# Sums and low parts of the feed-forward layers moved from GpSimd to VectorE in a two-layer decoder step

## The chip, the cores and the metric

The kernel runs on one core of a Trainium2 chip. The metric is the device time of one execution in microseconds; the time before is the median of three runs. A core has a matrix engine (TensorE, PE in the profile), three engines for elementwise work (VectorE = DVE, ScalarE = ACT, GpSimd = POOL), and queues that issue transfers (SyncE = SP, and here GpSimd too). Each engine works through its own instructions strictly in the order in which they stand; between engines they wait for each other by semaphores. SBUF is the working memory that all of them read; TensorE writes its results to PSUM, which VectorE and ScalarE read.

## The reference

One inference step of a two-layer decoder: 1024 new prompt tokens and 8 tokens of running sequences, model width 1024. Layer 0 has an mLSTM mixer, layer 1 latent attention with a paged cache, and after each mixer comes a dense SwiGLU feed-forward network (width 2816), where the change lies:

```python
def swiglu(x, w_gate_up, w_down):
    g, u = jnp.split(x @ w_gate_up, 2, axis=-1)
    return (jax.nn.silu(g) * u) @ w_down
...
hp = hp + swiglu(rmsnorm(hp, norm_ffn[layer]), ffn_w_gate_up[layer], ffn_w_down[layer])
```

Everything is float32.

## The kernel before

**Precision.** TensorE multiplies in a rounded format (fp32r). Each operand is therefore split in two: a high part, rounded by ScalarE (L117, the helper `split`), and a low part, source minus high part, which an elementwise engine makes at L118. A product is three matmuls: high by high (L134), high by low of the activations (L135), low of the weights by high (L136). `split` takes the engine of the low part as an argument; VectorE is the default.

**Seven products in place of eight.** The tokens are in four column groups: i = 0 and i = 1, of two halves each, 256 wide for i = 0 and 260 for i = 1 (`PW`). Both the gate/up product and the down product are made in 2x2 blocks with seven block products, of sums and differences of the blocks (`PRODUCTS`, in the order 0, 4, 3, 1, 2, 5, 6). So sums of weights and of activations have to be made, and split, ahead of the products:

- `operands` (L987 and following, per row block f of 128 rows, 22 of them): loads two weight tiles `wr` (L994, by SP), makes sums `S` on GpSimd (L1007, L1008, L1012, L1015), and splits seven weight operands.
- `gate_up`: for each f, seven products times two token groups, results in PSUM tiles `sc`; VectorE and ScalarE combine them into `u` (L1047 to L1061). The last product of an f completes `u[:, 1]` at L1061.
- `spread`: for a pair of row blocks (f0, f0+1), combinations of the four blocks of `u` in place, t1 (L1069), t2 (L1071), t3 (L1073) and t4 (L1075), and the splits into seven operands `b` for each token group. The table `SPREAD` says at which step of the down loop each is made: those of the next pair begin some 12 steps before the pair changes and end 4 steps after it.
- `down_raw`: loads a tile `dr` of down weights (L1087, by SP) and makes four sums `dS` of 128x128 (L1090 to L1093); `down_put` splits them and the raw block into `dA`, `dB`, `dC`, `dD`. Once for each of 4 blocks of output columns per pair and 10 pairs a layer: 40 down blocks a layer.
- `down`: for each down block 14 steps (seven products, two token groups), results in PSUM tiles `mm` and `ss`, combined into `wl` (i = 0) or `st` (i = 1) at L1129 to L1140, and at the end two transfers from GpSimd's queue that add the result to the residual in memory (`x_d`, L1141).
- the last two row blocks take another way (`last`), by plain products; four of their low parts are on GpSimd too.

**Order.** `down` is a generator: `gate_up` advances it by one step after every second k, so that the matmuls of gate/up for row block f stand between those of the down blocks of an earlier pair. A scheduler at compile time then sets the order of each engine's queue from the order of the code, the dependencies and its own estimates of durations; it moves instructions of all engines by some places. In the code before, `spread` has the low parts of operands 3 and 5 and the combination t2 on VectorE, and those of 0, 1, 2, 4, 6 and t1, t3, t4 on GpSimd; `down_raw` has all four sums on GpSimd.

Of the kernel before, what the change touches and what calls it, by code (L numbers as in the profile page):

```python
# [91 lines left out]
class Kern:  # L92
# [438 lines left out]
    def gates(self, p1, pg, gi, lf, bcol):  # L531
# [14 lines left out]
        b = self.t(pg, [8, S], "gb")  # L546
        G = self.t(pg, [8, S], "gG")
        wi = self.t(pg, [8, S], "gw")
# [7 lines left out]
        for c in range(NCK):  # L556
            s = slice(c * L, (c + 1) * L)
            V.tensor_tensor_scan(G[:, s], a[:, s], a[:, s], -BIG, op0=ALU.max, op1=ALU.max)
        ck = lambda x: x.rearrange("h (c l) -> h c l", l=L)
# [4 lines left out]
        V.tensor_copy(bL, last(b))  # L564
        V.tensor_tensor(aL, last(G), bL, op=ALU.add)
        V.memset(mm[:, 0:1], 0.0)
        V.tensor_tensor_scan(mm[:, 1:], bL, aL, 0.0, op0=ALU.add, op1=ALU.max)
        mp = mm[:, 0:NCK].unsqueeze(2).to_broadcast([8, NCK, L])
        V.tensor_tensor(ck(G), ck(G), mp, op=ALU.max)
        V.tensor_tensor(b, b, G, op=ALU.add)  # L570
        nc.scalar.activation(em, b, AF.Exp, scale=-1.0)
        V.tensor_tensor(ck(wi), mp, ck(G), op=ALU.subtract)
        nc.scalar.activation(wi, wi, AF.Exp)
# [488 lines left out]


    def spread(self, f0, n, i):
        V, G = self.nc.vector, self.nc.gpsimd
        a = self.u[f0, i]
        b = self.u.get((f0 + 1, i))
        if n == "t1":
            G.tensor_tensor(a[:, 0], a[:, 1], a[:, 0], op=ALU.subtract)  # L1069
        elif n == "t2":  # L1070
            V.tensor_tensor(a[:, 0], b[:, 1], a[:, 0], op=ALU.subtract)  # L1071
        elif n == "t3":
            G.tensor_tensor(a[:, 1], b[:, 1], a[:, 1], op=ALU.subtract)  # L1073
        elif n == "t4":
            G.tensor_tensor(b[:, 0], b[:, 0], a[:, 0], op=ALU.subtract)  # L1075
        else:
            x = a[:, n // 2] if n < 4 and n != 3 else a[:, 0] if n == 3 else b[:, n // 6]
            w = self.t(self.fp, [P, 2, PW[i]], f"b{n}{i}", F32R)
            self.split(w[:, 0], w[:, 1], x, lo_eng=V if n in (3, 5) else G)
            self.B[n, i] = w  # L1080


    def down_raw(self, wd, f0, dp):
        nc = self.nc
        G = nc.gpsimd.tensor_tensor
        raw = self.t(self.fp, [P, 2, 2 * P], "dr")
        nc.sync.dma_start(raw, self.wsrc(wd, f0 * P, 2, dp * 2 * P, 2 * P))  # L1087
        a11, a21, a12, a22 = (raw[:, k, r * P:r * P + P] for k in range(2) for r in range(2))
        S = self.t(self.fp, [P, 4, P], "dS")
        G(S[:, 1], a21, a22, op=ALU.add)  # L1090
        G(S[:, 0], S[:, 1], a11, op=ALU.subtract)
        G(S[:, 2], a11, a21, op=ALU.subtract)
        G(S[:, 3], a12, S[:, 0], op=ALU.subtract)  # L1093
        return {"A": raw[:, :, 0:P], "B": S[:, 0:2], "C": S[:, 2:4], "D": raw[:, 1:2, P:]}
# [59 lines left out]
    def ffn(self, layer):  # L1154
        wg, wd = self.ffn_w_gate_up[layer], self.ffn_w_down[layer]
        self.fp = self.pool("ffn")
        self.B = {}
        for _, x, i in SPREAD:
            if i == 0:
                self.spread(0, x, i)  # L1160
        self.gate_up(wg, 2, (0, 1))
        self.gate_up(wg, 0, (1,))
        self.gate_up(wg, 1, (1,))
        for _, x, i in SPREAD:
            if i == 1:
                self.spread(0, x, i)
        g = self.down(wd)
        next(g)
        self.gate_up(wg, 3, (0, 1), g, 1, 2)
        for f in range(4, NF - 1):  # L1170
            self.gate_up(wg, f, (0, 1), g)
        fs = range(NF - 2, NF)
        self.act = {}

        def last(pool, tag, i):
            for f in fs:
                if f not in self.act:
                    self.act[f] = [self.t(pool, [P, T], tag(f - NF + 2, x), F32R) for x in range(2)]
                o = lambda x: x[:, 512 * i:512 * i + 2 * PW[i]].rearrange("p (c t) -> p c t", c=2)
                self.split(o(self.act[f][0]), o(self.act[f][1]), self.u[f, i], lo_eng=(self.nc.gpsimd, self.nc.vector)[f % 2])  # L1180

        if layer:
            for i in range(2):
                self.gate_up(wg, NF - 1, (i,), g)
                last(self.fz, lambda j, x: f"f{2 * j + x}l", i)
            self.fc.release()
        else:
            self.gate_up(wg, NF - 1, (0, 1), g)
            self.fc.release()
            self.lt = self.pool("lt", side="right")  # L1190
            for i in range(2):
                last(self.lt, lambda j, x: f"l{j}{x}", i)
        for _ in g:
            pass
        return wd, fs
# [822 lines left out]
```

## Time and profile before

| | before |
|---|---|
| time, median of 3 runs | 2898.82 us (2897.31 to 2899.64) |
| profiled execution: time | 2918.12 us |
| profiled execution: span | 2916.0 us |
| mean granted TensorE clock | 0.946 |
| HBM read, written | 255.17 MB, 134.16 MB |

The page gives for each engine its busy time, its share of the span and its number of instructions; other views give the same for a stretch of time (windows), the waits of an engine by what ended them, and the instructions in order of time (timeline: start in us from the span's start, duration in us, engine, source line, operation, tile written <- tiles read, shape, and in brackets the idle time before it with what ended it). A granted clock of 1.00 is full speed. The two feed-forward networks lie at about 540 to 1290 us and 2095 to 2860 us of the span. Names of tiles lose their numbers in the profile.

### The profile page before, as it was taken

The numbers are of one execution on the slowest core, as the hardware profiler recorded it, in microseconds if no ns is written. First come the engines' busy times: TensorE is split into PE (matmuls) and PEld (weight loads), VectorE is DVE, ScalarE is ACT, GpSimd is POOL, SyncE is SP. The second block draws the span as 40 slices with busy tenths as digits, with TensorE's granted clock in tenths as the row PEclk, the third lists the DMA queues.
The fourth block names the chain that finished last, engine by engine and source line by source line (L and its number), as shares of the span: only waits on it lengthen the run. The fifth ranks groups of instructions, "written<-read, shape, count | busy, mean of one in ns | idle before, by whom it ended". The sixth has DMA issues, their size and how long they took to land.

```text
span 2916.0 us, 55167 instructions
## 1 busy us (share of the span) xinstructions
PE 2605.7 (89%) x21199; PEld 2438.1 (84%) x21199; DVE 1891.6 (65%) x3825; ACT 1357.2 (47%) x3403; POOL 1246.2 (43%) x1422
## 2 busy tenths in 40 slices
PE   8999989889889999989888888889979999989987
PEld 8998968889888989988875666677979888989986
DVE  4436678757666666666557777675766676666666
ACT  4213344455545555553354455454445545545543
POOL 1001012356655555542344454433156555555553
PEclk9999989999999999999899999999999999999998
DMA  5134455245555555573666765656316555555555
GB/s 175 44 72 106 120 146 150 80 99 106 113 107 106 106 103 106 114 176 109 215 227 223 262 239 195 204 178 196 120 54 121 102 102 106 112 108 108 113 127 139
DMA packets 346508, 392.91 MB, mean 135 GB/s; under 512 B 23833, under 2 KB 275102, under 8 KB 337926
## 3 DMA queue, kind: packets, MB, share of 16 engines
q0 software_dynamic: 63872, 191.79, 28.5%
q1 hardware_dynamic: 257974, 181.25, 20.9%
q10 hardware_dynamic: 24400, 16.36, 2.1%
q8 instruction: 166, 2.72, 0.4%
q14 instruction: 96, 0.79, 0.1%
HBM read 255.17 MB, written 134.16 MB: 134 GB/s over the span
## 4 chain that ended last, share of the span: by engine, by line
PE 53%; DVE 16%; DMA 10%; POOL 8%; issue 7%; ACT 5%; SPq 0%; another core or an unknown queue 0%; ACTq 0%; POOLq 0%; DVEq 0%
PE sc L134 9%; PE sc L136 9%; PE sc L135 9%; PE mm L134 4%; PE mm L136 4%; PE mm L135 4%; DMA wr<-in_ffn_w_gate_up_dram 3%; POOL b L118 2%; DVE tt L1796 2%; PE ss L1828 2%; DMA Gb<-G_d 2%; PE ss L134 1%; PE ss L135 1%; PE ss L136 1%; DVE b L118 1%
## 5 line engine op out<-in xcount | busy, mean ns | idle before, releaser
L117 ACT ACTIVATE wh<-wr 128x512 fp32r<-128x512 f32 (+3 forms) x176 | 139.0, 790 | 225.9 <-PE mm L135 129.4
L1141 POOL DMA_DIRECT2D x_d<-wl x80 | 96.1, 1202 | 324.0 <-DVE wl L1140 285.4
L118 POOL TENSOR_TENSOR b<-u,b 128x256 fp32r<-128x256 f32 (+1 forms) x200 | 176.5, 918 | 28.8 <-ACT b L117 28.8
L117 ACT ACTIVATE b<-u 128x256 fp32r<-128x256 f32 (+1 forms) x280 | 110.0, 413 | 119.2 <-POOL u L1073 40.1
L1796 DVE STREAM_TRANSPOSE tt<-nat 128x1024 f32<-128x1024 f32 x128 | 154.0, 1223 | 10.0 <-PE ss L1803 6.6
L118 DVE TENSOR_TENSOR wh<-S,wh 128x512 fp32r<-128x512 f32 x121 | 100.9, 834 | 66.1 <-ACT wh L117 65.6
L118 DVE TENSOR_TENSOR b<-u,b 128x256 fp32r<-128x256 f32 (+1 forms) x80 | 115.2, 1454 | 22.7 <-ACT b L117 22.7
L118 DVE TENSOR_TENSOR wl<-wr,wh 128x1024 fp32r<-128x1024 f32 (+2 forms) x83 | 99.2, 1197 | 41.5 <-ACT wh L117 27.3
L1007 POOL TENSOR_TENSOR S<-wr 128x512 f32<-128x512 f32 x45 | 63.7, 1415 | 128.1 <-DMA wr<-in_ffn_w_gate_up_dram 113.1
L1141 POOL DMA_DIRECT2D x_d<-st x80 | 109.4, 1368 | 4.8 <-issue 2.3
L134 PE MATMUL mm<-zh,wh 128*128 128x344 f32 x320 | 104.6, 327 | 5.7 <-DVE ot L462 5.7
L118 DVE TENSOR_TENSOR wh<-wr,wh 128x512 fp32r<-128x512 f32 x91 | 90.5, 996 | 29.4 <-ACT wh L117 28.8
L1803 PE MATMUL ss<-tt,qbd 128*32 128x128 f32 x2560 | 93.5, 281 | 15.9 <-DVE tt L1796 10.5
L135 PE MATMUL mm<-zl,wh 128*128 128x344 f32 x320 | 103.8, 325 | 0.0
L136 PE MATMUL mm<-zh,wl 128*128 128x344 f32 x320 | 103.7, 324 | 0.0
L118 DVE TENSOR_TENSOR dB<-dS,dB 128x256 fp32r<-128x256 f32 x80 | 58.8, 735 | 68.0 <-ACT dB L117 68.0
L1012 POOL TENSOR_TENSOR S<-S,wr 128x512 f32<-128x512 f32 x45 | 63.8, 1417 | 86.8 <-DVE wh L118 66.0
L1803 PEld LDWEIGHTS ss<-tt,qbd 128*32 128x32 f32 x2560 | 72.2, 112 | 32.6 <-DVE tt L1796 18.9
L850 POOL TENSOR_TENSOR ss<-ss,sq 128x512 f32<-128x512 f32 (+2 forms) x36 | 49.4, 1374 | 112.1 <-ACT sq L849 112.0
L117 ACT ACTIVATE wh<-S 128x512 fp32r<-128x512 f32 x121 | 76.2, 630 | 43.0 <-PE sc L136 24.4
L135 PE MATMUL mm<-b,dB 128*128 128x256 f32 (+1 forms) x160 | 48.9, 305 | 46.8 <-DVE b L118 46.8
L130 POOL TENSOR_TENSOR wl<-spl,wh 128x512 fp32r<-128x512 f32 x43 | 54.8, 1285 | 76.7 <-ACT spl L129 72.1
(1028 smaller groups left out, 11543.4 us busy)
## 6 DMA issues: line engine op xcount, KB each, us to landing
wr<-in_ffn_w_gate_up_dram SPq DMA_DIRECT2D x98, 512.0 KB
x_d<-st POOLq DMA_DIRECT2D x80, 520.0 KB
x_d<-wl POOLq DMA_DIRECT2D x80, 512.0 KB
dr<-in_ffn_w_down_dram SPq DMA_DIRECT2D x80, 256.0 KB
wr<-in_mlstm_w_in_dram SPq DMA_DIRECT2D x24, 512.0 KB
wr<-in_mlstm_w_out_dram SPq DMA_DIRECT2D x16, 512.0 KB
wr<-in_mla_w_o_dram SPq DMA_DIRECT2D x15, 512.0 KB
q<-qn_d SPq DMA_DIRECT2D x28, 256.0 KB
```

The costliest lines, as they stand in the source:

```text
L117: ins = nc.scalar.activation(hi, src, AF.Copy)
L118: self.low = e.tensor_tensor(lo, src, hi.bitcast(F32), op=ALU.subtract)
L130: nc.gpsimd.tensor_tensor(lo, x, hi.bitcast(F32), op=ALU.subtract)
L134: mm(ps, wh, xh, start=start, stop=False, **kw)
L135: mm(ps, wh, xl, start=False, stop=False, **kw)
L136: self.last = mm(ps, wl, xh, start=False, stop=stop, **kw)
L1007: G(s, a21, a22, op=ALU.add)
L1012: G(s, s, a11, op=ALU.subtract)
L1141: nc.gpsimd.dma_start(self.x_d[:, 2 * dp:2 * dp + 2, 512 * i:512 * i + 2 * PW[i]], st[i], accum_op=ALU.add)
L1796: V.transpose(out=tt, in_=src.rearrange("p s (c i) -> p c s i", i=32))
L1803: nc.tensor.matmul(psS[32 * j:32 * j + 32, u * P:u * P + P], self.qbd[:, b, cb], tt[:, c, 4 * j:4 * j + 4].rearrange("p s k -> p (s k)"), ...
L1828: nc.tensor.matmul(psV[32 * j:32 * j + 32], pz[:, j, i], keys[i // 4][:, j * 4 + i % 4], start=i == 0, stop=i == 7)
```

## The change

Three places. In `spread`, both names V and G now mean VectorE, and the split's low part is always there: per pair and token group t1, t3, t4 and the low parts of operands 0, 1, 2, 4 and 6. In `down_raw` the four sums are made by VectorE. In `ffn` (function `last`) two low parts per layer and token group, of which one was on GpSimd, are both on VectorE. GpSimd keeps the sums `S` of the gate/up weights and its transfers, and what it does outside these layers. The numbers computed are the same.

```diff
     def spread(self, f0, n, i):
-        V, G = self.nc.vector, self.nc.gpsimd
+        V = G = self.nc.vector
...
             w = self.t(self.fp, [P, 2, PW[i]], f"b{n}{i}", F32R)
-            self.split(w[:, 0], w[:, 1], x, lo_eng=V if n in (3, 5) else G)
+            self.split(w[:, 0], w[:, 1], x, lo_eng=V)
             self.B[n, i] = w
...
     def down_raw(self, wd, f0, dp):
         nc = self.nc
-        G = nc.gpsimd.tensor_tensor
+        G = nc.vector.tensor_tensor
...
-                self.split(o(self.act[f][0]), o(self.act[f][1]), self.u[f, i], lo_eng=(self.nc.gpsimd, self.nc.vector)[f % 2])
+                self.split(o(self.act[f][0]), o(self.act[f][1]), self.u[f, i], lo_eng=self.nc.vector)
```

In all 644 instructions go from GpSimd's queue to VectorE's: 200 low parts of `b`, 120 combinations, 320 sums of `dS` and four low parts of the last row blocks. The order of the engines around them changes with it. Two places are shown, both at the pair change near 1076 us of the profiled execution in layer 0 (u_11339 and u_11375 are the newer row block of the new pair, for the two token groups).

GpSimd's queue before, from the last combination of the pair to the last weight sums of the row block (b are low parts, dS_11786 the sums of the next down block):

```order
L1075 TENSOR_TENSOR u_11375<-u_11375,u_10975 128x260
L1090 TENSOR_TENSOR dS_11786<-dr_11784 128x128
L1092 TENSOR_TENSOR dS_11786<-dr_11784 128x128
L1091 TENSOR_TENSOR dS_11786<-dS_11786,dr_11784 128x128
L118 TENSOR_TENSOR b_11791<-u_10975,b_11791 128x260
L1093 TENSOR_TENSOR dS_11786<-dr_11784,dS_11786 128x128
L118 TENSOR_TENSOR b_11824<-u_11339,b_11824 128x256
L118 TENSOR_TENSOR b_11853<-u_11375,b_11853 128x260
L1012 TENSOR_TENSOR S_11720<-S_11720,wr_11716 128x512
L1015 TENSOR_TENSOR S_11720<-wr_11716,S_11720 128x512
```

GpSimd's queue now, for the same row block and the end of it:

```order
L1007 TENSOR_TENSOR S_11720<-wr_11718 128x512
L1008 TENSOR_TENSOR S_11721<-wr_11716,wr_11718 128x512
L1012 TENSOR_TENSOR S_11720<-S_11720,wr_11716 128x512
L1141 DMA x_d_91<-wl_6158 128x2x512
L1141 DMA x_d_91<-st_11542 128x2x520
L1015 TENSOR_TENSOR S_11720<-wr_11716,S_11720 128x512
L1141 DMA x_d_91<-wl_6157 128x2x512
```

The sums of weights now follow each other with only transfers between them, and L1015, which stood right behind L1012, stands behind two transfers.

VectorE's queue before, from the split of wh_11868 (weight of gate/up product 1) to that of wh_11872 (weight of product 3, made from L1012's sum):

```order
L118 TENSOR_TENSOR wh_11868<-S_11720,wh_11868 128x512
L118 TENSOR_TENSOR dC_11758<-dS_11551,dC_11758 128x256
L118 TENSOR_TENSOR b_11761<-u_10975,b_11761 128x260
L1131 TENSOR_TENSOR wl_6157<-wl_6157,ss_11776 128x256
L118 TENSOR_TENSOR b_11837<-u_11375,b_11837 128x260
L1049 TENSOR_TENSOR u_11765<-u_11765,sc_11813 128x256
L1131 TENSOR_TENSOR st_11777<-st_11777,ss_11779 128x260
L118 TENSOR_TENSOR dA_11884<-dr_11784,dA_11884 128x256
L118 TENSOR_TENSOR wh_11872<-S_11720,wh_11872 128x512
```

VectorE's queue now, the last part of the same stretch:

```order
L1092 TENSOR_TENSOR dS_11786<-dr_11784 128x128
L1091 TENSOR_TENSOR dS_11786<-dS_11786,dr_11784 128x128
L118 TENSOR_TENSOR b_11804<-u_11339,b_11804 128x256
L1093 TENSOR_TENSOR dS_11786<-dr_11784,dS_11786 128x128
L1131 TENSOR_TENSOR wl_6157<-wl_6157,ss_11776 128x256
L118 TENSOR_TENSOR b_11824<-u_11339,b_11824 128x256
L1131 TENSOR_TENSOR st_11777<-st_11777,ss_11779 128x260
L118 TENSOR_TENSOR b_11837<-u_11375,b_11837 128x260
L1049 TENSOR_TENSOR u_11765<-u_11765,sc_11813 128x256
L118 TENSOR_TENSOR b_11853<-u_11375,b_11853 128x260
L1049 TENSOR_TENSOR u_11807<-u_11807,sc_11842 128x260
L118 TENSOR_TENSOR wh_11872<-S_11720,wh_11872 128x512
```

From wh_11868 to wh_11872 there were seven instructions between the two; now there are 24. TensorE's order differs here by a few rows only: behind the first two matmuls with the high part of wh_11872 it now has six of the down product and one of the other token group before the first with the low part. SP's order is the same up to the last block of the program.

## The prediction

> **What bounds the kernel now.** I read the page first: busy time, share of the span and count by engine.
>
> ```profile
> PE 2605.7 (89%) x21199; PEld 2438.1 (84%) x21199; DVE 1891.6 (65%) x3825; ACT 1357.2 (47%) x3403; POOL 1246.2 (43%) x1422
> ```
>
> TensorE bounds it: VectorE and GpSimd are busy at 65% and 43%, so their sums matter only where TensorE stands still. The stretches of down blocks, by engine, come next (window and its length, TensorE, weight load, VectorE, ScalarE, GpSimd, granted clock), then TensorE's longest waits in the second of them (total, times, longest).
>
> ```profile
> 700.00:1280.00 580.00, 531.33 (x4243) 524.08 (x4243) 372.08 (x671) 298.05 (x803) 328.83 (x391) 0.95 0.55 110
> 2225.00:2830.00 605.00, 549.38 (x4363) 541.21 (x4364) 405.68 (x701) 309.53 (x837) 346.07 (x418) 0.94 0.54 106
> ```
>
> ```profile
> PE mm L135 <- DVE b L118: 30.0, 8, 5.1
> PE sc L134 <- ACT wh L117: 10.1, 5, 5.4
> PE sc L134 <- ACT w L117: 7.8, 3, 5.4
> ```
>
> TensorE idles 580−531.33 + 605−549.38 = 104.3 us there, in waits of up to 5.4 us. In order of time they come once per pair of feed-forward row blocks: two that I followed begin near 1006.4 and 1076.6 us, 70 us apart, so 580/70 makes 8 per stretch, 16 in all, 6.5 us each. VectorE and then GpSimd (timeline) at the first:
>
> ```profile
> 1004.59 6.81 DVE L118 TENSOR_TENSOR b<-u,b 128x260 fp32r<-128x260 f32 x1
> 1011.32 0.41 DVE L1131 TENSOR_TENSOR wl<-wl,ss 128x256 f32<-128x256 f32 x1
> 1011.65 0.42 DVE L118 TENSOR_TENSOR b<-u,b 128x260 fp32r<-128x260 f32 x1
> 1011.99 0.41 DVE L1049 TENSOR_TENSOR u<-u,sc 128x256 f32<-128x256 f32 x1
> ...
> 1013.40 0.69 DVE L118 TENSOR_TENSOR w<-S,w 128x512 fp32r<-128x512 f32 x1 [0.33 <-ACT w L117]
> 1014.01 0.42 DVE L1049 TENSOR_TENSOR u<-u,sc 128x260 f32<-128x260 f32 x1
> ```
>
> ```profile
> 1005.02 1.22 POOL L1075 TENSOR_TENSOR u<-u,u 128x260 f32<-128x260 f32 x1
> 1005.97 0.66 POOL L1090 TENSOR_TENSOR dS<-dr 128x128 f32<-128x128 f32 x1
> ...
> 1008.31 1.58 POOL L118 TENSOR_TENSOR b<-u,b 128x256 fp32r<-128x256 f32 x2
> 1009.68 1.42 POOL L1012 TENSOR_TENSOR S<-S,wr 128x512 f32<-128x512 f32 x1
> ```
>
> The same low part takes 0.42 us at 1011.65 and 6.81 us at 1004.59. The long one begins as GpSimd starts a run of nine instructions without a gap, all of which read SBUF tiles (L1075, the four sums of dS, three low parts, L1012; four rows of it are shown), and ends within 0.3 us of that run's end at 1011.1. Operations of VectorE that read one PSUM tile (L1131, L1049) keep 0.41 throughout. So what holds VectorE back is GpSimd's burst, and TensorE waits for the low part behind it. A second cost follows each wait: the granted clock, third column from the end, first just behind the wait of 1006.4, then behind two short waits that are used below:
>
> ```profile
> 1011.50:1018.00 6.50, 5.33 (x22) 0.51 0.19 54
> 2362.00:2366.00 4.00, 4.00 (x22) 0.59 0.00 0
> 2573.00:2577.00 4.00, 4.00 (x36) 1.00 0.00 0
> ```
>
> In the first row TensorE is busy 5.33 us at about half clock, so 2.6 us are lost; 16 times that is 42 us. The **pot** is 104 + 42 = 146 us.
>
> **The change, part by part.** Off GpSimd, onto VectorE:
>
> ```profile
> L118 POOL TENSOR_TENSOR b<-u,b 128x256 fp32r<-128x256 f32 (+1 forms) x200 | 176.5, 918 | 28.8 <-ACT b L117 28.8
> L118 DVE TENSOR_TENSOR b<-u,b 128x256 fp32r<-128x256 f32 (+1 forms) x80 | 115.2, 1454 | 22.7 <-ACT b L117 22.7
> L1092 POOL TENSOR_TENSOR dS<-dr 128x128 f32<-128x128 f32 x80 | 66.3, 829 | 0.0
> L1093 POOL TENSOR_TENSOR dS<-dr,dS 128x128 f32<-128x128 f32 x80 | 47.7, 596 | 3.0
> L1075 POOL TENSOR_TENSOR u<-u,u 128x256 f32<-128x256 f32 (+1 forms) x40 | 39.2, 981 | 1.4 <-DVE u L1071 1.4
> 1052.87 0.29 DVE L118 TENSOR_TENSOR dD<-dr,dD 128x128 fp32r<-128x128 f32 x1 [1.09 <-ACT dD L117]
> ```
>
> GpSimd loses 200 low parts (176 us), 4x80 down sums (48 to 66 us a group, some 229) and 3x40 combinations (some 110): about 510 of its 1246. VectorE's free pace comes from the starts above: 11.65 to 11.99 makes 0.34 us for 128x256, 13.40 to 14.01 makes 0.61 for 128x512; for 128x128 I take 0.29 less the 0.08 that the others overlap, 0.21. The 644 instructions cost VectorE 324x0.34 + 320x0.21 = 177 us. It gets much of that back, since the bursts that stretch its own instructions go: its 80 low parts take 1454 ns each against 420 for a free one, 83 us. I expect VectorE's total near today's.
>
> What decides is the pair change. I take the second of the two, at 1076.6, and walk VectorE's new queue from the second half's L1057 to the low part of wh_11872 (the weight of gate/up product 3, last of the order rows shown above), the operand that TensorE will wait for: 38 instructions, 3 of 128x512, 5 of 128x128, 30 of 128x256 or 128x260: 3x0.61 + 5x0.21 + 30x0.34 = 13.1 us. The rows of before that set its times:
>
> ```profile
> 1062.63 0.29 PE L136 MATMUL ss<-b,dB 128*128 128x260 f32 x1
> 1076.34 0.28 PE L136 MATMUL mm<-b,dB 128*128 128x260 f32 x1
> 1083.19 0.58 PE L134 MATMUL sc<-f3h,wh 128*128 128x256 f32 x1 [6.57 <-ACT wh L117]
> 1063.92 1.33 POOL L1008 TENSOR_TENSOR S<-wr,wr 128x512 f32<-128x512 f32 x1
> 1080.04 1.50 POOL L1012 TENSOR_TENSOR S<-S,wr 128x512 f32<-128x512 f32 x1
> 1064.07 1.72 DVE L118 TENSOR_TENSOR w<-wr,w 128x512 fp32r<-128x512 f32 x1 [0.98 <-ACT w L117]
> ```
>
> TensorE's products for L1057 are out at 1062.8, so VectorE starts at 1063.1. GpSimd's L1007 and L1008, which stay, hold its first low part until 1065.2, as the row at 1064.07 shows (+2.1). L1012 no longer stands behind eight instructions that have moved: it follows the low part of wh_11868, 13th of the 38 and near 1070.6, instead of starting at 1080.04, and costs VectorE 0.3. Each moved low part now waits in VectorE's queue for ScalarE's high part, with PSUM reads queued behind it; most are issued long after their high part, and I put 0.5 for the three or four that follow a combination at once. The sum is 1063.1 + 13.1 + 2.1 + 0.3 + 0.5 = 1079.1. TensorE reaches the first product of wh_11872 at 1076.4 and the first that needs its low part nine matmuls (of 0.12) later, at 1077.5. **A wait of 1.6 us stays** in place of 6.57. Bounds: with no hold at all VectorE is there at 1076.7, no wait; with all three sums held in full (3.9 in place of 2.4) and 1 us more each for ScalarE and for the transfer of dr, at 1082.6, 5.1 us.
>
> Does 1.6 us still halve the clock? The nearest rows:
>
> ```profile
> 2361.92 0.38 PE L134 MATMUL mm<-b,dD 128*128 128x256 f32 x1 [2.17 <-ACT wl L1135]
> 2572.65 0.39 PE L134 MATMUL mm<-b,dD 128*128 128x256 f32 x1 [1.87 <-ACT wl L1135]
> ```
>
> A wait of 2.17 us was followed by 0.59, one of 1.87 by 1.00 (windows above). I keep half of the 2.6 us. [...]
>
> The remaining steps: the two x_d transfers per block stay on GpSimd, with fewer instructions ahead. L1015, which frees wr for SP's next load, moves behind two of them, but runs near 1080 where it started at 1083.94, so SP loads no later; SP's order is otherwise the same up to the last block. The low parts at each layer's start add 11 instructions before the first weights, 11x0.34 = 3.7 us a layer at most, against waits of 3 us there that GpSimd's sums cause: I take 0, bounds -8 and +8. Cover for the moved down sums is VectorE's idle time; the rival below prices its loss.
>
> **Sum:** 16 x (1.6 + 1.3) = 46 of 146 us stay, so 100 us go: 2918.1 (profiled) to 2818. The median stands at 0.9934 of the profiled run, so about **2800 us**.
>
> **Rivals.**
> - *Nothing stays.* VectorE meets no hold; all 146 us go: 2754. For it: ten of the 38 read PSUM and are never held. Against: L1008 at 1063.92 visibly held one.
> - *VectorE is the new bound at the pair change.* It comes 4.5 us late and the clock still halves: 16 x (9.1 − 7.1) = 32 us gained, 2867. For it: 13.1 us of work in a stretch of 14.7. Against: the bound needs all delays at once.
> - *It isn't the burst.* If one holder at a time could block, an instruction could not wait 6.81 us, something else held it, and the waits stay: 2899. Against: the long wait ended with the burst, to 0.3 us. [...]
> - *Slower.* The down sums now stand in VectorE's queue behind a transfer: SP issues dr only after the low part of dD, and everything behind L1090 (weight low parts, PSUM reads) waits for it.
>
> ```profile
> 1040.02 0.37 SPq L1087 DMA_DIRECT2D dr<-in_ffn_w_down_dram  x1
> 1042.78 0.45 POOL L1090 TENSOR_TENSOR dS<-dr 128x128 f32<-128x128 f32 x1 [0.60 <-DMA dr<-in_ffn_w_down_dram]
> 1042.13 0.69 DVE L118 TENSOR_TENSOR wh<-S,wh 128x512 fp32r<-128x512 f32 x1 [1.50 <-ACT wh L117]
> ```
>
>  Landing takes 2.76 us; VectorE is free at 1040.6 and would wait 2.2 us, where GpSimd waited before. If TensorE paid that in each of 64 blocks, 141 us would be lost against 100 gained: 2940. It decides from 1.6 us a block. Against: VectorE idled 1.5 of those 2.2 us anyway (last row).
>
> **Chances.** Forecast 0.56, with its own range 2762 to 2843 (waits of 0.5 us, no halving, to 3 us with it); nothing stays 0.16; VectorE late 0.14; not the burst 0.05; slower 0.09. The range takes in the first three, 2748 to 2872. Faster by over 0.2% (what a measurement here can tell from no change) 0.86, within 0.05, slower 0.09.
>
> **What would show it.** Right: GpSimd near 740 us busy, VectorE near 1900; no VectorE low part over 3 us at a pair change; TensorE's waits there under 2 us; granted clock in the two stretches near 0.97. Wrong: those waits keep 5 us, behind a low part of wh or behind L1090; or VectorE waits for dr and TensorE for VectorE in every block.

## The result and the profile after

| | before | after |
|---|---|---|
| time, median (range) | 2898.07 us (2895.71 to 2899.64) | 2779.07 us (2775.64 to 2787.24) |
| ratio, with 95% interval | | 0.9594 (0.9572 to 0.9617) |
| profiled execution: time, span | 2918.12, 2916.0 us | 2787.24, 2785.5 us |
| mean granted TensorE clock | 0.946 | 0.962 |

119 us less by the medians, four runs of each. The page of the changed kernel, busy time by engine as before:

```profile
PE 2579.9 (93%) x21199; PEld 2412.7 (87%) x21199; DVE 1925.7 (69%) x4469; ACT 1352.1 (49%) x3403; POOL 859.2 (31%) x778
```

VectorE has 644 instructions more and is busy only 34 us longer; GpSimd loses 387 us. The two stretches of down blocks (they now begin and end earlier), and TensorE's longest waits in the first of them:

```profile
690.00:1222.00 532.00, 518.31 (x4263) 510.32 (x4261) 389.36 (x937) 297.03 (x806) 179.02 (x133) 1.00 0.60 121
2180.00:2695.00 515.00, 498.95 (x4072) 490.57 (x4071) 379.52 (x902) 285.08 (x778) 178.65 (x132) 0.99 0.59 117
```

```profile
PE sc L136 <- DVE wh L118: 6.0, 5, 1.2
PE sc L136 <- DVE w L118: 3.6, 3, 1.2
```

TensorE idles 13.69 + 16.05 = 29.7 us where it idled 104.3 (the second stretch here holds 4072 matmuls, the one before 4363), and the granted clock is 1.00 and 0.99 where it was 0.95 and 0.94. The waits of up to 6.6 us behind ScalarE's high parts and the low part of `b` are gone; one of 1.2 us per pair change stands in their place, behind the low part of `wh` or `w`. A pair change near 1040 us in order of time, VectorE first, then GpSimd, then TensorE at the end of its wait:

```profile
1031.96 1.52 DVE L1061 TENSOR_TENSOR u<-u,gt 128x260 f32<-128x260 f32 x1
1033.40 0.41 DVE L1140 TENSOR_TENSOR wl<-wl,ss 128x256 f32<-128x256 f32 x1
...
1038.52 0.41 DVE L1131 TENSOR_TENSOR st<-st,ss 128x260 f32<-128x260 f32 x1
1038.86 0.42 DVE L118 TENSOR_TENSOR b<-u,b 128x260 fp32r<-128x260 f32 x1
...
1040.20 0.68 DVE L118 TENSOR_TENSOR wh<-S,wh 128x512 fp32r<-128x512 f32 x1
```

```profile
1023.91 1.47 POOL L1007 TENSOR_TENSOR S<-wr 128x512 f32<-128x512 f32 x1 [5.43 <-DMA wr<-in_ffn_w_gate_up_dram]
1025.33 1.78 POOL L1008 TENSOR_TENSOR S<-wr,wr 128x512 f32<-128x512 f32 x1
1031.78 1.41 POOL L1012 TENSOR_TENSOR S<-S,wr 128x512 f32<-128x512 f32 x1 [4.67 <-DVE wh L118]
```

```profile
1040.94 0.38 PE L136 MATMUL sc<-f3h,wh 128*128 128x256 f32 x1 [1.20 <-DVE wh L118]
```

GpSimd's run of nine is gone; what is left of it, L1012 at 1031.78, holds one operation of VectorE with two SBUF inputs, L1061 at 1031.96, to 1.52 us in place of 0.42. VectorE then works without a gap until the low part of `wh` at 1040.20, for which TensorE waits. Over the whole program the low parts of `b`, all on VectorE now, go from 1454 ns to

```profile
L118 DVE TENSOR_TENSOR b<-u,b 128x256 fp32r<-128x256 f32 (+1 forms) x280 | 126.2, 456 | 18.0 <-ACT b L117 18.0
```

so 280 of them take about as long as 80 did.

### The profile page after: what moved, and what is told of

It reads as the page before. It is cut to its first block, busy times and chain, and to the rows that moved or that the text cites. A ratio compares the mean times of both kernels' runs of the same rounds, so it can differ in the third digit from the quotient of the medians.

```text
span 2785.5 us, 55009 instructions
## 1 busy us (share of the span) xinstructions
PE 2579.9 (93%) x21199; PEld 2412.7 (87%) x21199; DVE 1925.7 (69%) x4469; ACT 1352.1 (49%) x3403; POOL 859.2 (31%) x778
## 4 chain that ended last, share of the span: by engine, by line
PE 55%; DVE 24%; DMA 9%; ACT 4%; issue 4%; POOL 3%; SPq 0%; POOLq 0%; DVEq 0%; ACTq 0%
PE sc L136 10%; PE sc L134 10%; PE sc L135 10%; PE mm L134 4%; PE mm L136 4%; PE mm L135 4%; DVE b L118 3%; DVE tt L1796 2%; PE ss L1828 2%; DMA Gb<-G_d 2%; PE ss L134 1%; PE ss L136 1%; PE ss L135 1%; DVE wl L118 1%; DVE wh L118 1%
## 5 line engine op out<-in xcount | busy, mean ns | idle before, releaser
L1796 DVE STREAM_TRANSPOSE tt<-nat 128x1024 f32<-128x1024 f32 x128 | 153.7, 1222 | 14.6 <-DMA nat<-in_cache_latent_dram,idx 8.3
L1012 POOL TENSOR_TENSOR S<-S,wr 128x512 f32<-128x512 f32 x45 | 63.1, 1402 | 246.9 <-DVE wh L118 171.5
L118 DVE TENSOR_TENSOR b<-u,b 128x256 fp32r<-128x256 f32 (+1 forms) x280 | 126.2, 456 | 18.0 <-ACT b L117 18.0
L1015 POOL TENSOR_TENSOR S<-wr,S 128x512 f32<-128x512 f32 x45 | 75.8, 1685 | 119.6 <-DVE wh L118 79.2
L118 DVE TENSOR_TENSOR wh<-S,wh 128x512 fp32r<-128x512 f32 x121 | 86.4, 714 | 33.9 <-ACT wh L117 32.8
L1090 DVE TENSOR_TENSOR dS<-dr 128x128 f32<-128x128 f32 x80 | 52.1, 651 | 62.1 <-DMA dr<-in_ffn_w_down_dram 59.9
L1699 PE MATMUL mm<-wh,vt 128*128 128x256 f32 (+1 forms) x320 | 78.6, 307 | 9.9 <-ACT wh L117 5.0
L118 DVE TENSOR_TENSOR wh<-wr,wh 128x512 fp32r<-128x512 f32 x91 | 69.0, 758 | 23.4 <-ACT wh L117 22.8
L134 PE MATMUL sc<-zh,wh 128*128 128x344 f32 x256 | 84.1, 329 | 0.2 <-DVE q L432 0.2
L135 PE MATMUL sc<-zl,wh 128*128 128x344 f32 x256 | 83.1, 325 | 0.0
```

The costliest lines, as they stand in the source:

```text
L118: self.low = e.tensor_tensor(lo, src, hi.bitcast(F32), op=ALU.subtract)
L134: mm(ps, wh, xh, start=start, stop=False, **kw)
L135: mm(ps, wh, xl, start=False, stop=False, **kw)
L1012: G(s, s, a11, op=ALU.subtract)
L1015: G(s, a12, s, op=ALU.subtract)
L1699: nc.tensor.matmul(o, x, y, start=i == 0, stop=i == len(ops) - 1)
```

## The experiments

A measure used throughout: **held time**, the time of VectorE's two-input operations beyond what the same size takes free (0.28, 0.42 and 0.69 us for 128, 256 or 260, and 512 columns), counted where it is over 0.25 us, added up over the instruction records of 690 to 1222 us (first feed-forward layer) and 2180 to 2680 us (second). Ratios are to the kernel before on the same chip.

| run | time, us | ratio (95%) | held, first / second layer, us |
|---|---|---|---|
| before | | 1 | 89 / 89 |
| after | 2779.1 | 0.9594 (0.9572 to 0.9617) | 42 / 43 |
| e1_spread | 2797.6 | 0.9677 (0.9634 to 0.9719) | 57 / 63 |
| e2_down | 2888.1 | 0.9999 (0.9977 to 1.0021) | 109 / 102 |
| e3_reads | 2856.6 | 0.9877 (0.9838 to 0.9915) | 43 / 97 |
| e3_writes | 2821.3 | 0.9762 (0.9730 to 0.9794) | 43 / 38 |
| e3_writes_short | 2835.6 | 0.9820 (0.9786 to 0.9854) | 43 / 38 |
| e4_wsums_before | 2820.9 | 0.9763 (0.9723 to 0.9803) | 53 / 50 |
| e5_wsums_after | 2740.5 | 0.9476 (0.9450 to 0.9502) | 2 / 0 |
| e6_later | 2762.1 | 0.9550 (0.9522 to 0.9579) | 48 / 52 |
| e7_reads_clean | 2821.5 | 0.9763 (0.9728 to 0.9799) | 1 / 50 |
| e7_writes_clean | 2745.7 | 0.9496 (0.9455 to 0.9536) | 0 / 0 |
| e65_sums_later | 2740.9 | 0.9493 (0.9461 to 0.9525) | 1 / 0 |
| e8_down_on_gpsimd | 2758.2 | 0.9547 (0.9514 to 0.9579) | 17 / 17 |

### The two halves of the change: e1_spread, e2_down

e1_spread is the kernel before with the edit of `spread` alone:

```diff
-        V, G = self.nc.vector, self.nc.gpsimd
+        V = G = self.nc.vector
...
-            self.split(w[:, 0], w[:, 1], x, lo_eng=V if n in (3, 5) else G)
+            self.split(w[:, 0], w[:, 1], x, lo_eng=V)
```

e2_down is the kernel before with the edit of `down_raw` alone:

```diff
-        G = nc.gpsimd.tensor_tensor
+        G = nc.vector.tensor_tensor
```

> The kernel before with the moved work of the activation combinations alone (sums t1, t3, t4 and all low parts by VectorE); the four down sums per block stay on GpSimd. Theory (VectorE's operation with two SBUF inputs is held by GpSimd's unbroken burst at the pair change): the burst shrinks from nine instructions to the four down sums, about 2.9 us, so a hold of 6.8 us becomes one of at most 2.9 us; the wait at the pair change is 1 to 3 us, and the time about 2805 us (2780 to 2830). Rival (VectorE's own queue ahead of the low part is all that counts now): the four sums, 4 x 0.28 us, leave that queue, the wait falls from 1.2 to about 0.1 us and the time lies 15 to 20 us under the changed kernel, near 2760 us.

> The kernel before with the four down sums per block alone moved to VectorE; the combinations stay on GpSimd. Theory (burst): four of the nine instructions of the burst go, some 0.7 us each, so the hold falls from 6.8 to about 4 us; TensorE still waits about 3.5 us at each pair change and still runs at half clock behind it: 16 x 2.8 us gained, about 2850 us (2825 to 2885). Rival (it was the down sums that made GpSimd's burst unbroken, without them VectorE gets in between): almost the whole gain, 2780 to 2800 us.

**Measured.** e1_spread keeps four fifths of the gain. TensorE's waits in its first layer, and the 4 us behind one of them in the second (window row: TensorE busy, then weight load, the other engines, granted clock third from the end):

```profile
PE sc L136 <- DVE wh L118: 11.9, 5, 2.5
PE sc L136 <- DVE w L118: 6.0, 3, 2.0
```

```profile
2224.00:2228.00 4.00, 4.00 (x21) 4.00 (x22) 2.32 (x4) 1.49 (x5) 1.26 (x1) 0.57 0.74 176
```

The wait is 1.9 to 2.5 us, not 1.2, and a clock of 0.59 to 0.65 over 4 us follows it at six of the eight pair changes of the first layer. The burst theory said 1 to 3 us and about 2805; the rival, that only the length of VectorE's queue counts, said 2760. e2_down gains nothing, where the burst theory gave it some 45 us. VectorE and GpSimd at a pair change in its second layer, and TensorE's longest waits in the first:

```profile
2271.56 0.41 DVE L118 TENSOR_TENSOR dC<-dS,dC 128x256 fp32r<-128x256 f32 x1
2271.90 5.19 DVE L118 TENSOR_TENSOR b<-u,b 128x260 fp32r<-128x260 f32 x1
2277.01 0.28 DVE L1090 TENSOR_TENSOR dS<-dr 128x128 f32<-128x128 f32 x1
```

```profile
2272.32 1.22 POOL L1075 TENSOR_TENSOR u<-u,u 128x260 f32<-128x260 f32 x1
2273.03 2.55 POOL L118 TENSOR_TENSOR b<-u,b 128x260 fp32r<-128x260 f32 x3
2275.09 1.70 POOL L1012 TENSOR_TENSOR S<-S,wr 128x512 f32<-128x512 f32 x1
```

```profile
PE mm L135 <- DVE b L118: 28.5, 8, 3.9
```

**What follows.** A run of five GpSimd instructions holds one low part for 5.19 us, ending 0.3 us after the run. The run is shorter, but a low part is held for 5.2 to 5.6 us at all 16 pair changes, and the four down sums, L1090 among them, now stand behind it in VectorE's queue. So the 320 sums bring nothing while the rest of the burst is there. TensorE's waits on ScalarE's high parts of `wh` and `w` are down to 0.5 us here (in the kernel before up to 6.6), and that brings nothing either: the wait on the held low part has taken their place.

### Reads and writes on GpSimd: e3_reads, e3_writes, e3_writes_short

e3_reads adds to the changed kernel a helper, called in `spread` behind t1, t3, t4 and behind each split but those of operands 3 and 5, and in `down_raw` behind the sums (`self.w` is the pair of high and low part that was split last):

```diff
+    def extra(self, x, y):
+        if self.dm is not None:
+            self.nc.gpsimd.tensor_tensor(self.dm[:, :x.shape[-1]], x, y, op=ALU.subtract)
...
+            self.extra(self.w[:, 0], self.w[:, 1])
...
+        for k in range(4):
+            self.extra(S[:, k], S[:, 3 - k])
...
         self.fp = self.pool("ffn")
+        self.dm = self.ct[:, C_MM:C_MM + 3 * P] if layer else None
```

e3_writes has another body in the helper:

```diff
+            self.nc.gpsimd.tensor_copy(self.dm[:, 0:1], x[:, 0:1])
+            for _ in range(2):
+                self.nc.gpsimd.memset(self.dm[:, :3 * P if x.shape[-1] > P else 2 * P], 0.0)
```

and e3_writes_short shorter memsets in it:

```diff
+            for n in (3 * P, 16) if x.shape[-1] > P else (P,):
+                self.nc.gpsimd.memset(self.dm[:, :n], 0.0)
```

> The changed kernel, in whose second FFN layer GpSimd also makes tensor_tensor instructions of the old sizes in the old places, on data that VectorE has just made, into constants that nothing reads any more; no other instruction waits for their results. The first FFN layer is as in the changed kernel. Theory (GpSimd's reading of SBUF holds VectorE): the pair changes of the second layer lose 6 to 9 us again, 8 x 6 to 9 us, about 2840 us (2825 to 2860), with low parts of 4 to 7 us among VectorE's instructions. Rival (the moved results were late because GpSimd is slow at them): nobody waits for these results, so 2779 us, at most 10 us more.

> As the run with the added tensor_tensor instructions, but each of them is a copy of one column and two memsets (0.42 us each at 128x384, about 0.95 us together), so GpSimd's queue is as full for as long, and reads nothing but a column. Theory (reading of SBUF holds VectorE): within 10 us of the changed kernel, 2779 to 2790 us, low parts under 1 us. Rival (GpSimd's queue: its sums of the gate/up weights, L1012 and L1015, come late behind whatever fills it): as slow as the run with tensor_tensor instructions.

> As the run with copies and memsets, but cut to the time that the tensor_tensor instructions took (0.94 us for a low part or sum of the combinations, 0.54 us for a down sum; before, they took 1.3 and about 1.0 us, and GpSimd's weight sum L1012, behind them in the queue, came up to 9.4 us late for ScalarE). GpSimd's queue is now as full as in the run with tensor_tensor instructions and reads only columns. Theory (reading of SBUF holds VectorE): the time falls to 2780 to 2800 us, 2857 stays the price of the reads, and VectorE's low parts of b stay under 0.5 us on the mean. Rival (the filled queue): it stays near 2857 us, or at 2821.

**Measured.** The added reads take back seven tenths of the gain (0.9877 against 0.9594). Held time more than doubles in the second layer and stays in the first, which has none of them. No two-input operation there lasts over 2.1 us, though, where low parts of 4 to 7 us were expected. The groups of `b` on VectorE from 2180 to 2680 us, of e3_reads and then of e3_writes:

```profile
L118 DVE TENSOR_TENSOR b<-u,b 128x256 fp32r<-128x256 f32 (+1 forms) x98 | 60.6, 624 | 3.4 <-ACT b L117 3.4
```

```profile
L118 DVE TENSOR_TENSOR b<-u,b 128x256 fp32r<-128x256 f32 (+1 forms) x98 | 46.4, 475 | 6.1 <-ACT b L117 6.1
```

The writes leave VectorE as it was in the changed kernel (463 ns in the same stretch, held time 38 us). Yet both runs with writes are slower than the changed kernel, against the expectation. ScalarE's waits in e3_writes, then in e3_writes_short, say on what:

```profile
ACT wh L117 <- POOL S L1012: 33.7, 5, 9.4
```

```profile
ACT wh L117 <- POOL S L1012: 18.0, 5, 4.1
```

TensorE's longest wait in e3_writes is on ScalarE:

```profile
PE mm L134 <- ACT st L1144: 32.2, 7, 7.7
```

**What follows.** There are two prices. Reads hold VectorE (held time 97 us in the second layer with them, 38 with the writes). And the work that filled GpSimd's queue made its weight sum L1012 late, for which ScalarE waits, up to 9.4 us, with its own queue behind it, and then TensorE, up to 7.7. That was the rival, and it holds as well. With both in one kernel these three runs don't say what each is worth. Nor do they order the two runs with writes: in the shorter one a different wait grew, two of up to 7.6 us of TensorE on VectorE's L1146, and I did not follow it (VectorE waits up to 11.3 us for the transfer of `dr` there).

### The weight sums: e4_wsums_before, e5_wsums_after

One edit in `operands`, against the kernel before (e4_wsums_before) and against the changed one (e5_wsums_after):

```diff
-        G = nc.gpsimd.tensor_tensor
+        G = nc.vector.tensor_tensor
```

> The kernel before with the four sums of the gate/up weights (L1007, L1008, L1012, L1015) made by VectorE; combinations and down sums stay on GpSimd. Theory (burst): the run of nine instructions loses L1012, 1.4 us, and 2.6 us of L1007 and L1008 ahead of it; eight remain, a hold of 5 us; VectorE has four more operations of 0.6 us in its queue. About 2880 us (2860 to 2905). Rival (L1012's place at the end of GpSimd's queue, for which ScalarE and TensorE wait, is what costs the time): most of the gain, 2790 to 2820 us.

> The changed kernel with the four sums of the gate/up weights made by VectorE too: GpSimd is left with transfers. Theory (VectorE's queue ahead of the low part makes the wait of 1.2 us that stayed): three of the sums, 3 x 0.6 us, join that queue, the holds by L1007 and L1008 (about 1.1 us, the u<-u,gt of 1.52 us) go; the wait becomes 1 to 2.4 us, time 2785 us (2775 to 2800). Rival (the reads that GpSimd still makes are what is left of the loss): the waits go, 2755 to 2765 us.

**Measured.** Both went as the rivals said, e5_wsums_after further than its rival. e4_wsums_before gains 2.4% with the burst of combinations and down sums left in place. TensorE's waits from 2180 to 2680 us, before and then e4_wsums_before:

```profile
PE mm L135 <- DVE b L118: 19.9, 7, 5.1
PE sc L134 <- ACT wh L117: 8.9, 4, 5.4
PE sc L134 <- ACT w L117: 6.6, 2, 5.4
```

```profile
PE mm L135 <- DVE b L118: 12.7, 6, 3.9
PE mm L134 <- ACT wl L1135: 5.1, 5, 1.9
PE sc L134 <- ACT wh L117: 3.4, 5, 1.0
PE sc L134 <- ACT w L117: 2.0, 2, 1.0
```

The waits on ScalarE's high parts of `wh` and `w`, which are made from L1012's sum, fall from 5.4 to 1.0 us at the longest; VectorE is still held for up to 5.63 us. But the held time falls as well, from 89 to 53 and 50 us, so the run as a whole takes away some of both. The single pair changes tell them apart, by the starts of the same matmuls and by the longest low part of `b` in each. At six of the 16 a hold of 5.6 us is there in e4_wsums_before: they gain 0.7 to 2.9 us, 1.9 on the mean. At the other ten the longest is 2.1 us: they gain 3.2 to 6.7, 5.3 on the mean. At three of these ten (near 1222, 2518 and 2589 us in the kernel before) it was 1.9 us before too, so the hold is the same there, what went is the lateness of L1012, and they gain 6.1, 3.2 and 5.6 us. So the late L1012 was a cause of its own where the hold is short; where the long hold is there, moving L1012 brings little.

e5_wsums_after is the fastest kernel of the study: 2740.5 us, below both kernels compared here. Its page, and the group of `b` in its first layer:

```profile
PE 2550.0 (93%) x21199; PEld 2396.3 (87%) x21199; DVE 1906.2 (70%) x4649; ACT 1352.0 (49%) x3403; POOL 596.1 (22%) x598
```

```profile
L118 DVE TENSOR_TENSOR b<-u,b 128x256 fp32r<-128x256 f32 (+1 forms) x112 | 46.7, 422 | 0.9 <-ACT b L117 0.8
```

**What follows.** VectorE has 180 instructions more than after the change, each of 0.6 us, some 110 us of work, and is busy 19.5 us *less*: the holds that it loses cost it more than the work that it takes on. I had counted the three sums that join its queue and only 1.1 us of hold against them.

### The wait that stayed: e6_later, e65_sums_later

One edit in the table `SPREAD`, against the changed kernel (e6_later) and against e5_wsums_after (e65_sums_later):

```diff
-          (56, 2, 1), (57, 5, 0), (58, 6, 0), (59, 5, 1), (60, 6, 1))
+          (56, 2, 1), (61, 5, 0), (62, 5, 1), (63, 6, 0), (64, 6, 1))
```

> The changed kernel with the splits of operands 5 and 6 recorded four to five steps later (steps 61 to 64 in place of 57 to 60), so that three of their four low parts and one sum that reads PSUM stand behind the low part of the next pair's weight sum in VectorE's queue in place of ahead of it. Theory (that queue makes the wait of 1.2 us that stayed): 4 x 0.34 = 1.35 us leave it, the waits on wh and w go, with them what half clock is left: 16 x 1.2 to 1.6 us, 2757 us (2750 to 2765). Rival (the wait is set by something else, the high part or the weight sum): 2779 us, within 5 us.

> The kernel with the gate/up weight sums on VectorE too, and operands 5 and 6 split at steps 61 to 64. Theory (with GpSimd's reads gone VectorE is in time at the pair change): nothing left to gain there, 2740 us, within 6 us. Rival (VectorE's queue still sets the pair changes): 2722 to 2732 us.

**Measured.** e6_later has the time that was expected, 2762, and not the reason. TensorE's waits from 2190 to 2700 us:

```profile
PE sc L136 <- DVE wh L118: 6.7, 6, 1.3
PE mm L134 <- ACT wl L1135: 4.7, 4, 3.2
PE sc L136 <- DVE w L118: 3.7, 3, 1.3
```

The wait on `wh` and `w` is there as before. In the trace the same matmuls run 1.1 us earlier than in the changed kernel at 733 us and 3.4 us earlier at 1184 us, some 0.3 us per pair change where 1.2 were expected. In the second layer it is 9 us, 4 of them at one place near 2475 us, where the changed kernel runs at half clock (0.50 from 2474.5 to 2478.5 us); 11 of the 22 us by which the profiled execution is shorter fall between the layers, where nothing differs. The intervals of the ratios (0.9550 against 0.9594) just overlap. So the gain is not settled. Nor does the run decide whether the four instructions ahead of `wh` make the 1.2 us. VectorE's walk from the second half's L1057 to the end of that low part did get shorter, by 0.2 to 1.4 us at the eight pair changes of the first layer. But the compiled order of TensorE changed too: between its first matmul with the high part and its first with the low part there were eight others, now there is one, so TensorE comes to the low part 0.2 to 1.4 us sooner as well, and waits as long. e65_sums_later is the same as e5_wsums_after within the intervals, as expected: with the reads gone, the shift finds nothing to gain.

### The two prices apart: e7_reads_clean, e7_writes_clean, e8_down_on_gpsimd

The base is e5_wsums_after, where nothing but the output transfers stands in GpSimd's queue, so that added work there can make no sum late.

e7_reads_clean is e3_reads, and e7_writes_clean is e3_writes_short, both with the edit of `operands` above. e8_down_on_gpsimd has, against e5_wsums_after, the sums of `down_raw` (and the four low parts of `last`) where they were before:

```diff
-        G = nc.vector.tensor_tensor
+        G = nc.gpsimd.tensor_tensor
```

> The kernel in which VectorE also makes the gate/up weight sums (2740 us, GpSimd left with transfers), with GpSimd's tensor_tensor instructions of the old sizes and places added in the second layer, written over constants that nothing reads any more. Nothing waits for their results, and no weight sum stands behind them in GpSimd's queue now; only the output transfers do. Theory (reading of SBUF by GpSimd holds VectorE): VectorE's instructions of over 0.75 us come back in the second layer and only there (their excess from under 2 us to 40 to 60 us), and the time rises by 20 to 60 us, to about 2780 us. Rival (only what stands behind the added work in GpSimd's queue costs time): at most 2750 us.

> The same base, with a one-column copy and memsets of the same time in place of each added tensor_tensor instruction in the second layer. Theory (reads hold, writes don't; a filled queue costs time only through what stands behind it): within 8 us of 2740 us, and VectorE has next to no instruction of over 0.75 us. Rival (any work of GpSimd on SBUF holds VectorE): as slow as the run with the reads.

> Combinations and gate/up weight sums on VectorE, the down sums alone on GpSimd as before. Theory (holds by what GpSimd still reads): four reads of about 0.7 us in a row at each of the 40 down blocks of a layer hold one operation of VectorE for up to 2.8 us; at the pair change that is a wait of 1 to 2 us again: 2740 + 16 x 1 to 2 us, about 2760 us (2748 to 2775). Rival (VectorE gains more from the 320 sums less, 320 x 0.21 us, than the holds cost): 2725 to 2740 us.

**Measured.** The second layer, 2180 to 2680 us, of the run with reads and then of the run with writes: the stretch by engine (GpSimd's busy time is the fifth), and the group of `b`:

```profile
2180.00:2680.00 500.00, 458.59 (x3620) 448.01 (x3619) 382.05 (x856) 251.60 (x688) 227.78 (x283) 0.96 0.54 108
```

```profile
2180.00:2680.00 500.00, 484.64 (x4004) 480.13 (x4002) 366.11 (x957) 280.42 (x764) 243.26 (x691) 0.99 0.61 123
```

```profile
L118 DVE TENSOR_TENSOR b<-u,b 128x256 fp32r<-128x256 f32 (+1 forms) x104 | 61.7, 599 | 0.0
```

```profile
L118 DVE TENSOR_TENSOR b<-u,b 128x256 fp32r<-128x256 f32 (+1 forms) x110 | 45.7, 420 | 0.0
```

GpSimd is busy 228 us with the reads and 243 with the writes. With the writes TensorE gets 4004 matmuls through in these 500 us, with the reads 3620. The time is 2745.7 us with writes, the same as without them within the intervals, and 2821.5 with reads: 76 us more for work of like length. All of it arises in the second layer: the starts of the same matmuls in the two traces differ by some 5 us at most up to 2040 us, and by over 70 at the layer's end. I had put the reads at 20 to 60 us; with 50 us of held time the granted clock falls too (0.96 against 0.99).

**What follows.** That reading of SBUF by GpSimd is what holds VectorE is shown: beside the reads a low part takes 599 ns on the mean and 50 us of held time come up in the layer, beside writes that keep GpSimd busy for as long it takes 420 ns and there is none. Which of VectorE's operations are held shows in the kernel before: of its two-input operations in the two stretches of the table, none of the 594 with a PSUM input lasts over 0.43 us, and those on SBUF alone last up to 6.8.

e8_down_on_gpsimd costs 18 us over e5_wsums_after, with 17 us of held time in each layer, close to the theory's 2760. But no two-input operation lasts over 1.54 us, where holds of up to 2.8 were expected, and a wait of 1 to 2 us at each pair change isn't there. By the starts of the same matmuls the first layer loses 5 us and the second 15 (4 come back between them). TensorE's waits from 2140 to 2700 us in this run, and the first of these two in e5_wsums_after (2190 to 2700 us):

```profile
PE sc L134 <- ACT wh L117: 4.3, 3, 1.4
PE ss L134 <- DVE st L1131: 3.0, 5, 0.6
```

```profile
PE sc L134 <- ACT wh L117: 0.8, 3, 0.3
```

The three waits of 1.4 us are at pair changes, and in the 4 us behind each the granted clock is 0.57 or 0.58.

## Why the prediction came out as it did

The forecast was 2800 us with a range of 2748 to 2872; 2779 was measured. Step by step:

- **The sum of the 16 pair changes: right, in part by luck.** By the starts of the same matmuls in the two traces, eight pair changes gain 50.5 us in the first layer and 49.9 in the second, 100.4 together, where 100 was predicted. What stays at each was made up differently, as the next bullets show.
- **The walk of VectorE's queue: right to 0.8 us.** 16.0 us were worked out from the second half's L1057 to the end of the low part of `wh`; at the pair change shown it starts at 1024.11 and ends at 1040.88, 16.8. L1012's hold was put at 0.3 and is 1.1 (the L1061 of 1.52 us), and there are 39 instructions in that stretch, not 38. TensorE arrives later too, so the wait is 1.2 us, predicted 1.6.
- **Half of the clock loss kept: wrong, next to none stays.** Behind the wait at 1040.9 and most others there is none:

```profile
1040.90:1044.90 4.00, 3.96 (x33) 3.96 (x34) 1.68 (x4) 2.12 (x6) 2.29 (x1) 1.00 0.57 111
```

  Behind 14 of the 16 waits of 1.2 us the granted clock is 1.00; behind the other two it is 0.50 (2474.5 to 2478.5 us) and 0.57 (2603 to 2607 us), and behind the wait of e1_spread's second layer shown above (waits of up to 2.5 us) 0.57 as well. So the length of a wait alone, by which I had halved the loss, does not tell in these runs whether it follows. What is left of the loss per pair in the first layer is some 3 us by the distance of the pair changes: 63.0 us, against 60 by my estimate of 504 matmuls at 0.119 us, the median distance of their starts. It is the 1.2, one of about 0.5 in every third, and many under 0.5, which I had not counted. The two errors cancel, and that is luck.
- **The layer starts: the mis-sized term.** I took 0 with bounds of 8 us. Each layer gains 8 to 9 us ahead of the first of the eight pair changes (by the starts of the same matmuls, at times of the kernel before: from +0.5 us at 557 to −8.1 at 660, and from −74.2 at 2154 to −83.2 at 2229), some 17 us in all. A ninth pair change lies there, ahead of the windows from which I counted 16, and 5.5 us of each layer's gain fall at it: the count should have been 18. Of the start's own waits one falls from 2.97 to 0.77 us in the first layer. This is nearly all of the 21 us between 2800 and 2779.
- **Profiled execution and median.** The profiled executions differ by 131 us, the medians by 119: some 15 us of the difference lie in the attention part between the layers, which the change doesn't touch. 100 + 17 come close to the medians' 119.
- **Engine totals: VectorE right, GpSimd off.** VectorE 1926 (1900 predicted), GpSimd 859 (740). I subtracted durations, and on GpSimd these overlap: L1075 of 1005.02 lasts 1.22 us and the next starts at 1005.97. Nothing hung on it.
- **The cause: half of it.** That the burst is the cause stands, and that its reads hold VectorE is now shown (e7). But I put down TensorE's waits to the held low part, with the late L1012 as a remark. TensorE's waits of the first stretch before (700 to 1280 us), and the low part at a pair change near 874 us:

```profile
PE sc L134 <- ACT wh L117: 19.5, 5, 6.6
PE mm L135 <- DVE b L118: 16.6, 7, 5.1
PE sc L134 <- ACT w L117: 11.8, 3, 5.4
```

```profile
866.69 1.95 DVE L118 TENSOR_TENSOR b<-u,b 128x260 fp32r<-128x260 f32 x1
```

  At nine of the 16 pair changes the long wait is on the held low part, at seven (the one of 1076.6 that I walked among them) on a high part that ScalarE makes from L1012's sum. At six of these seven the low part lasted 2.0 us at most, though at four of the six GpSimd's nine instructions ran without a gap as well. The burst had two ways to TensorE: VectorE held, and the sum at its end late for ScalarE. Either alone keeps most of the loss: e2_down has the second nearly gone (0.5 us at the longest) and gains nothing (0.9999), and e4_wsums_before gains little where the long hold is (1.9 us a pair change on the mean). The change removes both at once, which is why the sum came out all the same.
- **The rivals.** "Not the burst" falls by e7. "Slower", with the down sums waiting for `dr` in VectorE's queue: the wait came, and was hidden. VectorE's waits of the first stretch have it 14 times, 2.3 us at most, and among TensorE's there none is on an operand made from these sums:

```profile
DVE dS L1090 <- DMA dr<-in_ffn_w_down_dram: 21.8, 14, 2.3
```

  "Nothing stays", 2754, needed the remaining reads to go as well: e5_wsums_after does that and reaches 2740.
- **What stays open.** What makes the 1.2 us. e6_later shortens VectorE's walk and TensorE's way to it alike. In e5_wsums_after the wait is gone with GpSimd's last reads, but the orders of VectorE and TensorE differ there too: the walk is no shorter (15.2 to 16.3 us in the first layer, 14.9 to 16.8 after the change), and TensorE comes to the low part later. Open too is why, beside the same unbroken run of GpSimd, the low part is held for 2 us at some pair changes and for 6.8 at others.

## What to carry to other kernels

GpSimd, slower than VectorE (before, a low part took 918 ns on it on the mean, and 0.42 us on VectorE when nothing held it) and far from being the bound (43% busy), cost more here through what it took from VectorE and through one late sum than through the rest of its work: look for single operations of VectorE that last many times their usual time (here 6.81 us in place of 0.42), and for what GpSimd reads meanwhile. Where two waits end at the same place, as the held low part and the late sum did, removing one may show nothing (e2_down, 0.9999). Before handing VectorE more work, subtract the time that it is held; here it took on 824 operations in all (the 644, and 180 weight sums) and was busy 15 us longer than at the start, for 5% of the time. In these runs work on GpSimd that wrote and read no more than a column did VectorE no harm (e7_writes_clean, no held time), and in e3_writes it still harmed what stood behind it in GpSimd's queue (L1012, for which ScalarE waited up to 9.4 us).

## What the runs showed of the hardware that was not expected

- One VectorE operation, a low part that took 0.42 us elsewhere, lasted until 0.3 us after the end of a whole unbroken run of GpSimd instructions: 6.81 us beside nine (1004.59 us of the kernel before) and 5.19 us beside five (2271.90 us of e2_down). It didn't always: at four pair changes of the kernel before, beside an unbroken run of the same nine, it lasted 2.0 us at most and ended 0.3 us after the first of them. In e7_reads_clean, where GpSimd waits on VectorE's results now and then, no two-input operation lasts over 1.31 us in the second layer, yet the held time is 50 us in a layer.
- VectorE's two-input operations with a PSUM input were not held: 0.43 us at most for 594 of them before, while those on SBUF alone lasted up to 6.8 us.
- GpSimd's copy of one column took 0.28 to 0.34 us on the mean (2180 to 2680 us of e3_writes, e3_writes_short and e7_writes_clean), and two memsets of 384 columns 0.90 together (e3_writes, at 2217.75 us). This short work added up: in e3_writes ScalarE waited up to 9.4 us for L1012 behind it.
